# Reciprocal roots of a two-block transformer kernel: a power on GpSimd in the place of ScalarE's root and VectorE's reciprocal

## The chip, the cores and the metric

The kernel runs on one core of a Trainium2 chip. The time is that of one execution on the device, in microseconds (us), and the median of several runs is compared. TensorE (PE in the profile) multiplies and transposes, VectorE (DVE) and ScalarE (ACT) work on rows of 128 partitions, GpSimd (POOL) does small work and issues some loads, and SyncE (SP) issues the loads of the weights. All of them read and write the on-chip SBUF; PE's products land in PSUM. ACT evaluates a function from a table, and an ACT_TABLE_LOAD stands ahead of a function whose table isn't the one in place.

## The reference

Input are 256 tokens of width 1024, in fp32. A first block (one layer) mixes them by attention, by a long convolution (hyena) and by a Fourier branch, adds a mixture of 16 experts where each expert picks its top 32 tokens, and ends in a norm. A second block follows, of two layers. Every norm is of this form:

```python
def rms_norm(x, g):
    y = x * lax.rsqrt(jnp.mean(x * x, axis=-1, keepdims=True) + EPS)
    return y * g

def second_block(...):
    for i in range(2):
        f = swiglu(rmsnorm(h, g[0]), gate[i, 0], up[i, 0], down[i, 0])
        h = h + 0.5 * rmsnorm(f, g[1])
        mix = hybrid_mixer(rmsnorm(h, g[2]), ...)
        h = h + rmsnorm(mix, g[3])
        f = swiglu(rmsnorm(h, g[4]), gate[i, 1], up[i, 1], down[i, 1])
        h = h + 0.5 * rmsnorm(f, g[5])
        gate_ = sigmoid(rmsnorm(h, g[6]) @ w_ple_gate[i])
        h = h + rmsnorm((p[i] @ w_ple[i]) * gate_, g[7])
```

In the first block `qk_heads` norms each head of 64, the router works on the norm of the residual, and in the second block's mixer the latents (256 and 128 wide) and both groups of the attention output (512 wide) are normed too.

## The kernel before

Tokens stand on the partitions, in two halves of 128. Weights stream from HBM in 1 MB tiles through a ring of slots that SP refills. Except in the experts, a product keeps fp32 accuracy by splitting each operand in a high and a low part: `wsplit` copies a piece of 128 x 1024 of a weight on ACT (`wh`, line 1137) and subtracts on DVE (`wl`, line 1138), or on POOL for the first eight pieces of the second block, and `mm3` (lines 163 to 165) multiplies three times.

The first mixer runs to about 300 us; `head_norm` (line 484) norms the heads, and beside it POOL multiplies by the rope's cosines (`ho`, line 497). The router follows, half by half (line 798): ACT squares the residual and sums (`sqj`, 814), takes the root (`rr`, 816), DVE its reciprocal (817); ACT takes the exponential of the logits (`affw`, 830), and x times `rr` (`x1h`, `xs`, 896 and 897) is what the tokens are gathered from. The top 32 of each expert are found from `affw`, then the tokens are gathered, and the products of the experts begin, for which 384 loads of 1 MB stream in to 1256 us. A first Sqrt of one element (`warm`, line 972) follows the last expert's Silu.

The second block is eight sublayers long: FFN, mixer, FFN and embedding gate (PLE), twice. Each ends in `rows_linear` (line 1202), whose first half of the tokens ends eight weight tiles before the second, so that the chain of norms of one half runs beside the products of the other. For a half, `between` (line 1181) does this:

- ACT squares the result and sums (`ns`, 1155), DVE multiplies by the gain (`nt`, 1194), ACT takes the root (1158 or 1160), DVE the reciprocal (1161)
- DVE adds it to the residual (`x`, 1195)
- `pre_norm_half` (1164) repeats it for the next norm: Square (1155), product with the gain (1169), root and reciprocal; then DVE scales the rows in two pieces (1172), PE transposes them (eight `tr`, 1175), ACT and DVE split them into `hh` and `hl` (1178, 1179)

Lines 1011 and 1013 add the experts' result and apply the first block's last norm. At the very end `last_half` (line 1336) treats the second half's result by columns; its root is warmed by a Sqrt of one element (line 1353). Each engine works its instructions in a fixed order, which the scheduler of the build chose from estimated times; where a cost changes, it places instructions anew. POOL's instructions are in one queue, in which subtractions, loads of gains (`gain`, line 1073) and rope products stand together.

Of the kernel before, what the change touches and what calls it, by code (L numbers as in the profile page):

```python
# [11 lines left out]
F32 = mybir.dt.float32  # L12
F32R = mybir.dt.float32r
I32 = mybir.dt.int32
AF = mybir.ActivationFunctionType
# [18 lines left out]
def _constants():  # L34
# [3 lines left out]
    # rows of the axial rope, interleaved pairs  # L38
# [6 lines left out]
    # implicit filter features and decay  # L45
# [9 lines left out]
    # real DFT of 512 points on 256 samples: cos | -sin with the Nyquist row in the place of sin 0  # L55
# [13 lines left out]
    # 2-d DFT of the Fourier branch, ortho  # L69
# [9 lines left out]
    # masks of the second block: causal, and ln of the number of dilated windows that hold a pair  # L79
# [24 lines left out]
class Builder:  # L104
# [28 lines left out]
    def slot(self, i, nm, dt=F32):  # L133
        """one of the two halves of what becomes the experts' tokens"""
# [5 lines left out]
    def load(self, view, src):  # L140
        """next tile of the weight stream"""
# [25 lines left out]
    def rstd(self, pool, ss, n, width, tag="rs"):  # L167
        """1 / sqrt(ss / width + eps) of a [128, n] tile"""
        nc = self.nc
        r = pool.tile([128, n], F32, name=tag, tag=tag)  # L170
        nc.scalar.activation(r, ss, AF.Sqrt, bias=self.eps, scale=1.0 / width)
        nc.vector.reciprocal(r, r)
        return r

    def sumsq(self, pool, junk, src, n_out=1, tag="ss"):
        nc = self.nc
        s = pool.tile([128, 1], F32, name=tag, tag=tag)
        nc.scalar.activation(junk, src, AF.Square, accum_out=s)
        return s

    def sin_reduced(self, pool, r, x, shape, tag):
        """r = x reduced to [-pi, pi] by multiples of 2 pi"""
# [12 lines left out]
    def run(self):  # L195
# [7 lines left out]
        nc.vector.memset(self.eps, EPS)  # L203
        self.ones = P.tile([128, 128], F32, name="ones")
# [25 lines left out]
    def first_mixer(self, st):  # L230
        nc, tc, A = self.nc, self.tc, self.A
        P, M, ident = self.P, self.M, self.ident
        # left: what lives to the end of the phase | the middle's operands; right: tokens | branches
# [28 lines left out]
        # small vectors as rows, then as columns  # L262
# [29 lines left out]
        # silu of both conditionings; 16 equal columns each  # L292
# [5 lines left out]
        # modulation: columns of 2048 at a time, four column tiles of the array at once  # L298
# [36 lines left out]
        # norms of x and ctx, transposed  # L335
        def norm_T(src, dst, scaled):
            for h in range(2):
                xn = scaled(h)
                s = self.sumsq(L, xn, src[:, h])
                r = self.rstd(L, s, 1, D)  # L340
# [8 lines left out]
        def affine(i, src, hi, lo):  # L349
            """src (1 + scale) g + shift, split"""  # L350
# [22 lines left out]
        # affine of the norms: A = g (1 + sc), B = sh  # L373
# [22 lines left out]
        # implicit filters  # L396
# [22 lines left out]
        # spectra: A = re, B = im (row 0 zero), Dm = re with the Nyquist row first; [f, (order, w)]  # L419
# [11 lines left out]
        # 1 / sum |filter|, channels on the partitions  # L431
# [10 lines left out]
        # rope tables with the gains of q and k  # L442
# [15 lines left out]
        def by_k(w):  # L458
            """pieces of a [128, 8, 256] chunk for products with the tokens on the rows"""
# [23 lines left out]
        def head_norm(src, nh):  # L483
            """rms norm over 64 of each of nh heads, [128, nh, 64] in PSUM"""
            sq = H1.tile([128, 8, 64], F32, name="hsq", tag="hsq", bufs=1)
            nc.scalar.activation(sq[:, :nh], src, AF.Square)
            ss = H1.tile([128, 8], F32, name="hss", tag="hss", bufs=2)
            nc.vector.tensor_reduce(ss[:, :nh], sq[:, :nh], axis=AX.X, op=OP.add)
            r = self.rstd(L, ss[:, :nh], nh, 64, tag="hr%d" % nh)
# [15 lines left out]
        def twice(nh, o, t):  # L505
            """o + t, each head two times, for transposes that fill the lower and the upper rows"""
# [73 lines left out]
        # hyena columns: padded, short convolution  # L580
# [12 lines left out]
        # Fourier columns  # L593
# [3 lines left out]
        # operands of the branch products: attention 4, hyena 2, Fourier 2  # L597
# [15 lines left out]
        # attention over 256 + 256 keys, heads i of both groups together  # L613
# [39 lines left out]
        # hyena: two long convolutions  # L653
# [41 lines left out]
        # Fourier mix  # L695
# [41 lines left out]
        # gates and branches, 256 features at a time; the other modulations in between  # L737
# [37 lines left out]
        # router weights with the gain of norm 2, and what its shift brings to the logits  # L775
# [12 lines left out]
        # output product, half by half  # L788
# [9 lines left out]
        def router(h):  # L798
            """the residual, and the affinities of its norm to the experts"""
# [14 lines left out]
            nc.scalar.activation(junk, x[:, h], AF.Square, accum_out=s)  # L814
            r = rr[h] = B.tile([128, 1], F32, name="rr", tag="rr", bufs=2)
            nc.scalar.activation(r, s, AF.Sqrt, bias=self.eps, scale=1.0 / D)
            nc.vector.reciprocal(r, r)
# [35 lines left out]
        # operands of the gather: they outlive this phase a little  # L853
# [816 lines left out]
```

## Time and profile before

| | us |
|---|---|
| runs: median (lowest to highest) | 2371.19 (2369.87 to 2372.92) |
| profiled execution: span | 2373.4 |
| PE busy | 1985.2 (84%) |
| DVE busy | 924.2 (39%) |
| ACT busy | 768.6 (32%) |
| POOL busy | 94.9 (4%) |
| mean DMA rate | 276 GB/s |

The profiled execution took as long as the slowest of the runs. The shares are of the whole span, through which three stretches run with different limits; so the rows further down are taken stretch by stretch. In them a line gives the start and the length of an instruction, then engine, line of the kernel, operation, what is written and what is read, and in square brackets how long the engine had been idle and who released it.

### The profile page before, as it was taken

The page shows a single profiled execution, that of the slowest core. Times are in us where ns is not written, and L with a number is a line of the kernel's source. Part 1 is how long each engine was busy: PE and PEld are TensorE (multiplying, and loading weights), DVE is VectorE, ACT ScalarE, POOL GpSimd, SP SyncE. Part 2 cuts the span into 40 slices and gives each one's busy share as a digit, 9 for nine tenths or more (in the row PEclk, how much of TensorE's full clock was granted, in tenths as well). Part 3 has the DMA queues.
Part 4 walks back from the last instruction along what each step waited for, and adds up shares of the span by engine and source line. Part 5 has one row for each costly group of instructions (what it writes and reads, how often), then busy time and mean ns, then how long its engine had stood idle before and what let it go on. Part 6 is the DMA issues. An engine that isn't in the chain of part 4 may idle for free.

```text
span 2373.4 us, 32208 instructions
## 1 busy us (share of the span) xinstructions
PE 1985.2 (84%) x13512; PEld 1344.9 (57%) x13512; DVE 924.2 (39%) x1535; ACT 768.6 (32%) x1235; POOL 94.9 (4%) x110
## 2 busy tenths in 40 slices
PE   7899977666666666666666999999999999999998
PEld 4778932111111111111114998879987998879986
DVE  5855530100000000000005555676547554777545
ACT  5544420000000000000003444576436544666444
POOL 2100010000000000000003000100000000110000
PEclk9999987767766776677677999999999999999999
DMA  9466699999999999999996654437556554536551
GB/s 327 151 230 215 248 358 417 416 416 417 417 417 416 417 416 417 417 417 416 417 417 218 213 179 155 154 113 228 179 185 205 178 194 141 172 127 196 178 194 64
DMA packets 234869, 655.78 MB, mean 276 GB/s; under 512 B 12663, under 2 KB 143140, under 8 KB 198884
## 3 DMA queue, kind: packets, MB, share of 16 engines
q1 hardware_dynamic: 230436, 639.00, 71.6%
q0 software_dynamic: 4288, 14.72, 1.9%
q8 instruction: 106, 1.74, 0.3%
q14 instruction: 39, 0.32, 0.0%
HBM read 650.54 MB, written 3.15 MB: 275 GB/s over the span
## 4 chain that ended last, share of the span: by engine, by line
PE 55%; DMA 37%; DVE 4%; ACT 3%; issue 1%; SPq 0%; DVEq 0%; POOL 0%; ACTq 0%; POOLq 0%
DMA wt<-in_w_up_dram 24%; DMA wt<-in_w_down_dram 12%; PE gu L163 8%; PE gu L165 8%; PE gu L164 8%; PE acc L163 5%; PE acc L165 5%; PE acc L164 5%; PE gu L942 2%; PE mm L163 2%; PE mm L165 1%; PE mm L164 1%; PE mod L310 1%; ACT wh L1137 1%; PE gu L1593 1%
## 5 line engine op out<-in xcount | busy, mean ns | idle before, releaser
L1138 DVE TENSOR_TENSOR wl<-wt,wh 128x1024 fp32r<-128x1024 f32 (+1 forms) x380 | 462.6, 1223 | 295.9 <-ACT wh L1137 295.1
L942 PE MATMUL gu<-wt,xg 128*32 128x512 f32 x2048 | 392.0, 860 | 190.3 <-DMA wt<-in_w_up_dram 97.5
L1137 ACT ACTIVATE wh<-wt 128x1024 fp32r<-128x1024 f32 x388 | 404.6, 1051 | 302.9 <-PE gu L164 118.6
L942 PEld LDWEIGHTS gu<-wt,xg 128*32 128x32 f32 x2048 | 50.5, 126 | 517.0 <-DMA wt<-in_w_up_dram 231.6
L163 PE MATMUL gu<-hh,wh 128*128 128x256 f32 x1152 | 326.3, 283 | 0.0
L164 PE MATMUL gu<-hl,wh 128*128 128x256 f32 x1152 | 326.0, 283 | 0.0
L165 PE MATMUL gu<-hh,wl 128*128 128x256 f32 x1152 | 326.0, 283 | 0.0
L967 ACT ACTIVATE a<-gu 128x512 f32<-128x512 f32 x16 | 9.6, 597 | 865.6 <-PE gu L942 865.6
L990 PE MATMUL tr<-wt,aT 128*32 128x256 f32 x2048 | 193.0, 525 | 96.7 <-DMA wt<-in_w_down_dram 84.1
L973 DVE TENSOR_TENSOR a<-a,gu 128x512 f32<-128x512 f32 x16 | 11.0, 688 | 561.6 <-PE gu L942 559.5
L164 PEld LDWEIGHTS gu<-hl,wh 128*128 128x128 f32 x1152 | 221.1, 192 | 0.0
L165 PEld LDWEIGHTS gu<-hh,wl 128*128 128x128 f32 x1152 | 221.1, 192 | 0.0
L163 PEld LDWEIGHTS gu<-hh,wh 128*128 128x128 f32 x1152 | 221.1, 192 | 0.0
L990 PEld LDWEIGHTS tr<-wt,aT 128*32 128x32 f32 x2048 | 71.2, 140 | 211.7 <-DMA wt<-in_w_down_dram 142.7
L163 PE MATMUL acc<-wh,ah 128*128 128x512 f32 x352 | 139.8, 397 | 0.0
L165 PE MATMUL acc<-wh,al 128*128 128x512 f32 x352 | 139.6, 396 | 0.0
L164 PE MATMUL acc<-wl,ah 128*128 128x512 f32 x352 | 139.5, 396 | 0.0
L995 DVE TENSOR_TENSOR y<-tr,g2b 32x256 f32<-32x256 f32 x64 | 26.9, 420 | 278.3 <-PE tr L990 277.6
L163 PE MATMUL acc<-wh,hh 128*128 128x256 f32 (+1 forms) x304 | 102.4, 337 | 1.1 <-ACT vd L1408 1.1
L163 PE MATMUL gu<-wh,hh 128*128 128x256 f32 (+1 forms) x336 | 99.8, 298 | 0.4 <-ACT hh L1178 0.4
L165 PE MATMUL acc<-wh,hl 128*128 128x256 f32 (+1 forms) x304 | 99.6, 328 | 0.0
L164 PE MATMUL acc<-wl,hh 128*128 128x256 f32 (+1 forms) x304 | 99.1, 326 | 0.0
(456 smaller groups left out, 2889.7 us busy)
## 6 DMA issues: line engine op xcount, KB each, us to landing
wt<-in_w_gate_dram SPq DMA_DIRECT2D x128, 1024.0 KB, 19.8
wt<-in_w_up_dram SPq DMA_DIRECT2D x128, 1024.0 KB, 19.9
wt<-in_w_down_dram SPq DMA_DIRECT2D x128, 1024.0 KB, 20.0
wt<-in_ffn_gate_dram SPq DMA_DIRECT2D x44, 1024.0 KB, 6.3
wt<-in_ffn_up_dram SPq DMA_DIRECT2D x44, 1024.0 KB, 5.4
wt<-in_ffn_down_dram SPq DMA_DIRECT2D x44, 1024.0 KB, 4.9
wt<-in_w_in_dram SPq DMA_DIRECT2D x35, 1024.0 KB, 5.4
wt<-in_w_mod_dram SPq DMA_DIRECT2D x24, 1024.0 KB, 8.5
```

Of the source, the lines that this page charges most:

```text
L163: mm(out, lw[0], rw[0], start=start, stop=False, skip_group_check=skip)
L164: mm(out, lw[0], rw[1], start=False, stop=False, skip_group_check=skip)
L165: mm(out, lw[1], rw[0], start=False, stop=stop, skip_group_check=skip)
L310: last = mm(ps[32 * j:32 * j + 32, :], cst[:, k].rearrange("p a b -> p (a b)"), w[:, 512 * j:512 * j + 512], start=(k == 0), stop=(k == KD ...
L942: mm(ps[32 * j:32 * j + 32, :], xg[k][:, 32 * e:32 * e + 32], w[:, 512 * j:512 * j + 512], start=(k == 0), stop=(k == KD - 1), skip_group_ ...
L967: silu = nc.scalar.activation(a, pga, AF.Silu)
L973: mul = nc.vector.tensor_tensor(a, a, pup, op=OP.mult)
L990: mm(pd[32 * c:32 * c + 32, :256], aT[:, b, 32 * j:32 * j + 32], w[:, i, 256 * c:256 * c + 256], start=(t == 0), stop=(t == 15), skip_grou ...
L995: nc.vector.tensor_tensor(y4[32 * r:32 * r + 32, 256 * c:256 * c + 256], pd[32 * c:32 * c + 32, :256], self.g2b[32 * c:32 * c + 32, 256 * ...
L1137: nc.scalar.activation(hi, src, AF.Copy)
L1138: (eng or nc.vector).tensor_tensor(lo, src, hi.bitcast(F32), op=OP.subtract)
L1593: mm(p[:, e * i:e * i + e], q(n0 + i, h), k(n0 + i, e), start=True, stop=True, skip_group_check=True)
```

## The change

All norms but the group norm of the mixer (its root, line 1547, stays on ACT) take their reciprocal root on POOL. A new function does it in two instructions, an add of epsilon and a power with the exponent -0.5 from a constant tile:

```diff
+    def root(self, r, ms, eps=EPS):
+        self.nc.gpsimd.tensor_scalar(r, ms, eps, None, op0=OP.add)
+        self.nc.gpsimd.tensor_tensor(r, r, self.mhalf[:, :r.shape[-1]], op=OP.pow)
...
+        self.mhalf = P.tile([128, 8], F32, name="mhalf")
+        nc.vector.memset(self.mhalf, -0.5)
...
     def norm_rstd(self, src, junk, width, half=False):
+        f = 2.0 if half else 1.0
-        nc.scalar.activation(junk, src, AF.Square, accum_out=s)
+        nc.scalar.activation(junk, src, AF.Square, scale=f * width ** -0.5, accum_out=s)
-            nc.scalar.activation(r, s, AF.Sqrt, bias=self.eps4, scale=4.0 / width)
...
-            nc.scalar.activation(r, s, AF.Sqrt, bias=self.eps, scale=1.0 / width)
-        nc.vector.reciprocal(r, r)
+        self.root(r, s, f * f * EPS)
...
-            nc.scalar.activation(sq[:, :nh], src, AF.Square)
+            nc.scalar.activation(sq[:, :nh], src, AF.Square, scale=0.125)
...
-            nc.scalar.activation(r, s, AF.Sqrt, bias=self.eps, scale=1.0 / D)
-            nc.vector.reciprocal(r, r)
+            self.root(r, s)
...
-                    nc.scalar.activation(warm, self.eps, AF.Sqrt)
...
-                nc.scalar.activation(s[:, 2:3], self.eps, AF.Sqrt)
...
-            nc.scalar.activation(s[:, 3:4], s[:, 0:1], AF.Sqrt, bias=self.eps, scale=1.0 / D)
+            self.root(s[:, 3:4], s[:, 0:1])
             nc.vector.tensor_tensor(t[:, cs], t[:, cs], g[:, cs], op=OP.mult)
-            nc.vector.reciprocal(s[:, 3:4], s[:, 3:4])
```

The division by the width goes into the scale of the Square. In the order of ACT 50 roots and the two of one element are gone, and 25 ACT_TABLE_LOADs stand where 48 stood; on DVE 50 reciprocals are gone; on POOL 100 instructions are new. Other instructions move, since the scheduler places them anew.

On ACT, in the second half of the router (`sqj` the square of the residual, `rr` the root, `affw` the exponential, `x1h` and `xs` the rows for the gather), it read:

```order
L814 ACTIVATE sqj,rss<-x_70 128x1024
L816 ACT_TABLE_LOAD
L816 ACTIVATE rr<-rss,eps 128x1
L897 ACTIVATE xs<-x_70,rr 128x1024
L830 ACT_TABLE_LOAD
L830 ACTIVATE affw,rsum<-lg,rm 128x16
L896 ACTIVATE x1h<-x_70,rr 128x1024
L897 ACTIVATE xs<-x_70,rr 128x1024
```

and reads now:

```order
L815 COPY xt<-tr 128x512
L818 ACTIVATE sqj,rss<-x_72 128x1024
L900 ACTIVATE xs<-x_72,rr 128x1024
L899 ACTIVATE x1h<-x_72,rr 128x1024
L833 ACTIVATE affw,rsum<-lg,rm 128x16
L900 ACTIVATE xs<-x_72,rr 128x1024
```

The root and the table loads around it are gone, and the rows for the gather go ahead of the exponential.

On POOL, where the second block begins (`wl` the subtractions for the first weights, `gain` loads of norm gains), it read:

```order
L1029 DMA grows<-in_norm_gains_dram 1x16x64
L1138 TENSOR_TENSOR wl<-wt,wh 128x1024 x7
L1073 DMA gain<-in_norm_gains_dram 128x1024
L1138 TENSOR_TENSOR wl<-wt,wh 128x1024
L1073 DMA gain<-in_norm_gains_dram 128x1024
```

and reads now, the roots of the four norms of this place between them:

```order
L1027 DMA grows<-in_norm_gains_dram 1x16x64
L1134 TENSOR_TENSOR wl<-wt,wh 128x1024 x2
L169 TENSOR_SCALAR nr<-ns 128x1
L170 TENSOR_TENSOR nr<-nr,mhalf 128x1
L1134 TENSOR_TENSOR wl<-wt,wh 128x1024 x2
L169 TENSOR_SCALAR nr<-ns 128x1
L170 TENSOR_TENSOR nr<-nr,mhalf 128x1
L169 TENSOR_SCALAR nr<-ns 128x1
L170 TENSOR_TENSOR nr<-nr,mhalf 128x1
L1134 TENSOR_TENSOR wl<-wt,wh 128x1024
L1069 DMA gain<-in_norm_gains_dram 128x1024
L1134 TENSOR_TENSOR wl<-wt,wh 128x1024
```

The first root stands behind two subtractions and the next two behind four; the last of the four comes after this piece.

On DVE, at the border of the second FFN of layer 0 and the PLE product, the first half of the tokens (`nt` the rows, `nr` the reciprocal root, `wl` subtractions of the running product's weights), it read:

```order
L1194 TENSOR_TENSOR nt<-acc,gain 128x1024
L1161 RECIPROCAL nr<-nr 128x1
L1195 SCALAR_TENSOR_TENSOR x_70<-nt,nr,x_70 128x1024
L1138 TENSOR_TENSOR wl<-wt,wh 128x1024
L1169 TENSOR_TENSOR nt<-x_70,gain 128x1024
L1138 TENSOR_TENSOR wl<-wt,wh 128x1024
L1161 RECIPROCAL nr<-nr 128x1
L1138 TENSOR_TENSOR wl<-wt,wh 128x1024
L1172 TENSOR_SCALAR nt<-nt,nr 128x512 x2
L1138 TENSOR_TENSOR wl<-wt,wh 128x1024 x2
```

and reads now:

```order
L1187 TENSOR_TENSOR nt<-acc,gain 128x1024
L1188 SCALAR_TENSOR_TENSOR x_72<-nt,nr,x_72 128x1024
L1134 TENSOR_TENSOR wl<-wt,wh 128x1024
L1162 TENSOR_TENSOR nt<-x_72,gain 128x1024
L1134 TENSOR_TENSOR wl<-wt,wh 128x1024
L1165 TENSOR_SCALAR nt<-nt,nr 128x512 x2
L1134 TENSOR_TENSOR wl<-wt,wh 128x1024
```

The reciprocals are gone, and the scaling of the rows has one subtraction fewer ahead of it. In PE's order the eight transposes that follow it have moved ahead of 8 matmuls of the running product here; at the other borders of the second block they moved by 8 to 10 matmuls ahead in seven more halves, by one in two, and not at all or behind up to 8 in the others.

## Rows read from the trace of the kernel before

**Rows 1.** Windows: busy time of each engine and instructions, granted clock, DMA share, GB/s

```profile
300.00:1256.00 956.00, 635.92 (x4277) 151.96 (x4277) 69.01 (x159) 28.01 (x46) 9.22 (x11) 0.71 1.01 414
...
1256.00:2373.00 1117.00, 1075.45 (x7316) 972.68 (x7316) 676.56 (x1011) 594.34 (x964) 61.72 (x60) 0.98 0.52 171
```

**Rows 2.** Waits of PE, 1256 to 2374 us: total us, times, longest us

```profile
PE tr L1175 <- DVE nt L1172: 17.6, 5, 10.5
```

**Rows 3.** Groups by line: busy us, mean ns, then idle before

```profile
L1160 ACT ACTIVATE nr<-ns,eps 128x1 f32<-128x1 f32 x25 | 7.2, 286 | 0.3
...
L1161 DVE RECIPROCAL nr<-nr 128x1 f32<-128x1 f32 x33 | 5.2, 156 | 4.9 <-ACT nr L1160 3.4 <-ACT nr L1158 1.5
```

**Rows 4.** Timeline, first mixer: start us, duration us, instruction, count

```profile
20.41 1.28 ACT L405 ACT_TABLE_LOAD   x1
...
59.79 2.14 POOL L497 TENSOR_TENSOR ho<-hn,tabc 128x512 f32<-128x512 f32 x1 [8.72 <-issue]
```

**Rows 5.** Timeline: small POOL instructions, and the DVE ones beside them

```profile
47.02 3.70 DVE L1138 TENSOR_TENSOR wl<-wt,wh 128x1024 fp32r<-128x1024 f32 x3
...
47.04 1.32 POOL L454 TENSOR_TENSOR tabs<-k_ropes,gains 128x32 f32<-128x32 f32 x1
...
50.80 0.26 POOL L454 TENSOR_TENSOR tabs<-k_ropes,gains 128x32 f32<-128x32 f32 x1
...
299.77 0.19 POOL L861 COPY gaff<-aff 128x8 f32<-128x8 f32 x1 [126.95 <-DVE yt L805]
```

**Rows 6.** Timeline of ACT in the second half of the router

```profile
303.43 1.28 ACT L816 ACT_TABLE_LOAD   x1
...
304.93 1.13 ACT L897 ACTIVATE xs<-x,rr 128x1024 f32<-128x1024 f32 x1
...
307.37 0.31 ACT L830 ACTIVATE affw<-lg,rm 128x16 f32<-128x16 f32 x1
```

**Rows 7.** Window ahead of the experts' stream

```profile
319.00:323.00 4.00, 4.00 (x24) 1.51 (x20) 0.00 (x0) 0.46 (x1) 0.00 (x0) 0.56 0.50 152
```

**Rows 8.** Timeline from the experts into the second block: POOL, DVE, PE

```profile
1267.02 11.40 POOL L1138 TENSOR_TENSOR wl<-wt,wh 128x1024 fp32r<-128x1024 f32 x4 [1.51 <-ACT wh L1137]
...
1273.84 4.87 DVE L1172 TENSOR_SCALAR nt<-nt,nr 128x512 f32<-128x512 f32 x2
...
1276.36 1.09 PE L1175 MATMUL tr<-ident,nt 128*128 128x128 f32 x4 [10.55 <-DVE nt L1172]
...
1287.87 1.38 PE L1175 MATMUL tr<-ident,nt 128*128 128x128 f32 x8 [2.43 <-DVE nt L1172]
```

**Rows 9.** Timeline, gate product into the next layer: ACT, DVE, PE

```profile
1815.91 1.28 ACT L1160 ACT_TABLE_LOAD   x1
...
1817.73 1.28 DVE L1195 SCALAR_TENSOR_TENSOR x<-nt,nr,x 128x1024 f32<-128x1024 f32 x1
...
1824.16 1.77 PE L1175 MATMUL tr<-ident,nt 128*128 128x128 f32 x8 [3.20 <-DVE nt L1172]
```

**Rows 10.** Timeline: POOL in the mixer, and one half border of the second block

```profile
1478.49 1.84 POOL L1515 MEMSET qz<- 128x2048 f32 x1
...
1786.95 1.28 ACT L1158 ACT_TABLE_LOAD   x1
...
1786.97 1.22 DVE L1194 TENSOR_TENSOR nt<-acc,gain 128x1024 f32<-128x1024 f32 x1 [10.07 <-ACT nt L1155]
...
1788.77 1.28 DVE L1195 SCALAR_TENSOR_TENSOR x<-nt,nr,x 128x1024 f32<-128x1024 f32 x1
...
1794.58 0.87 DVE L1172 TENSOR_SCALAR nt<-nt,nr 128x512 f32<-128x512 f32 x2
...
1795.46 1.04 PE L1175 MATMUL tr<-ident,nt 128*128 128x128 f32 x8
```

**Rows 11.** Timeline of DVE at the end

```profile
2367.51 0.68 DVE L1357 TENSOR_TENSOR nt<-nt,gain 128x512 f32<-128x512 f32 x1
...
2368.37 1.41 DVE L1361 SCALAR_TENSOR_TENSOR x<-nt,ls,x 128x512 f32<-128x512 f32 x2
```

More of the change, by code (lines that the diff above doesn't have):

```diff
@@ L165, in mm3, with rstd, meansq @@
         mm(out, lw[1], rw[0], start=False, stop=stop, skip_group_check=skip)
-    def rstd(self, pool, ss, n, width, tag="rs"):
-        nc = self.nc
+    def root(self, r, ms, eps=EPS):
+        self.nc.gpsimd.tensor_scalar(r, ms, eps, None, op0=OP.add)
+        self.nc.gpsimd.tensor_tensor(r, r, self.mhalf[:, :r.shape[-1]], op=OP.pow)
+    def rstd(self, pool, ms, n, tag="rs"):
         r = pool.tile([128, n], F32, name=tag, tag=tag)
-        nc.scalar.activation(r, ss, AF.Sqrt, bias=self.eps, scale=1.0 / width)
-        nc.vector.reciprocal(r, r)
-        return r
-    def sumsq(self, pool, junk, src, n_out=1, tag="ss"):
-        nc = self.nc
+        self.root(r, ms)
+        return r
+    def meansq(self, pool, junk, src, tag="ss"):
         s = pool.tile([128, 1], F32, name=tag, tag=tag)
-        nc.scalar.activation(junk, src, AF.Square, accum_out=s)
+        self.nc.scalar.activation(junk, src, AF.Square, scale=D ** -0.5, accum_out=s)
         return s
@@ L338, in norm_T @@
                 xn = scaled(h)
-                s = self.sumsq(L, xn, src[:, h])
-                r = self.rstd(L, s, 1, D)
+                r = self.rstd(L, self.meansq(L, xn, src[:, h]), 1)
                 nc.vector.tensor_scalar(xn, src[:, h], r, None, op0=OP.mult)
@@ L485, in head_norm @@
             sq = H1.tile([128, 8, 64], F32, name="hsq", tag="hsq", bufs=1)
-            nc.scalar.activation(sq[:, :nh], src, AF.Square)
+            nc.scalar.activation(sq[:, :nh], src, AF.Square, scale=0.125)
             ss = H1.tile([128, 8], F32, name="hss", tag="hss", bufs=2)
             nc.vector.tensor_reduce(ss[:, :nh], sq[:, :nh], axis=AX.X, op=OP.add)
-            r = self.rstd(L, ss[:, :nh], nh, 64, tag="hr%d" % nh)
+            r = self.rstd(L, ss[:, :nh], nh, tag="hr%d" % nh)
             n = H1.tile([128, 8, 64], F32, name="hn", tag="hn", bufs=1)
@@ L813, in router @@
             junk = B.tile([128, D], F32, name="sqj", tag="xt", bufs=2)
-            nc.scalar.activation(junk, x[:, h], AF.Square, accum_out=s)
+            nc.scalar.activation(junk, x[:, h], AF.Square, scale=D ** -0.5, accum_out=s)
             r = rr[h] = B.tile([128, 1], F32, name="rr", tag="rr", bufs=2)
-            nc.scalar.activation(r, s, AF.Sqrt, bias=self.eps, scale=1.0 / D)
-            nc.vector.reciprocal(r, r)
+            self.root(r, s)
             p = tps()
@@ L967, in moe @@
             silu = nc.scalar.activation(a, pga, AF.Silu)
-            if e == NE - 1:
-                warm = self.G.tile([128, 1], F32, name="warm")
-                with tc.issue_after(silu.ins):
-                    nc.scalar.activation(warm, self.eps, AF.Sqrt)
             mul = nc.vector.tensor_tensor(a, a, pup, op=OP.mult)
@@ L1058, in rest @@
             nc.vector.tensor_copy(self.gcol, p[:, :16])
-            self.eps4 = C.tile([128, 1], F32, name="eps4")
-            nc.vector.memset(self.eps4, 4.0 * EPS)
             self.fg, self.g0 = [C.tile([128, D], F32, name="gain", tag="gain", bufs=2) for _ in range(2)]
@@ L1153, in norm_rstd @@
         nc = self.nc
+        f = 2.0 if half else 1.0
         s = self.G.tile([128, 1], F32, name="ns", tag="ns", bufs=4)
-        nc.scalar.activation(junk, src, AF.Square, accum_out=s)
+        nc.scalar.activation(junk, src, AF.Square, scale=f * width ** -0.5, accum_out=s)
         r = self.G.tile([128, 1], F32, name="nr", tag="nr", bufs=4)
-        if half:
-            nc.scalar.activation(r, s, AF.Sqrt, bias=self.eps4, scale=4.0 / width)
-        else:
-            nc.scalar.activation(r, s, AF.Sqrt, bias=self.eps, scale=1.0 / width)
-        nc.vector.reciprocal(r, r)
+        self.root(r, s, f * f * EPS)
         return r
@@ L1344, in tail @@
             cs = slice(512 * c, 512 * c + 512)
-            sig = nc.scalar.activation(t[:, cs], acc, AF.Sigmoid)
+            nc.scalar.activation(t[:, cs], acc, AF.Sigmoid)
             nc.vector.tensor_tensor(t[:, cs], t[:, cs], pw[:, cs], op=OP.mult)
             if c == 0:
-                nc.scalar.activation(fg[:, cs], t[:, cs], AF.Square, accum_out=s[:, 0:1])
+                nc.scalar.activation(fg[:, cs], t[:, cs], AF.Square, scale=D ** -0.5, accum_out=s[:, 0:1])
                 nc.gpsimd.tensor_tensor(t[:, cs], t[:, cs], g[:, cs], op=OP.mult)
                 return
-            with self.tc.issue_after(sig.ins):
-                nc.scalar.activation(s[:, 2:3], self.eps, AF.Sqrt)
-            nc.vector.tensor_tensor_reduce(fg[:, cs], t[:, cs], t[:, cs], 1.0, 0.0, OP.mult, OP.add, s[:, 1:2])
+            nc.vector.tensor_tensor_reduce(fg[:, cs], t[:, cs], t[:, cs], 1.0 / D, 0.0, OP.mult, OP.add, s[:, 1:2])
             nc.vector.tensor_tensor(s[:, 0:1], s[:, 0:1], s[:, 1:2], op=OP.add)
-            nc.scalar.activation(s[:, 3:4], s[:, 0:1], AF.Sqrt, bias=self.eps, scale=1.0 / D)
+            self.root(s[:, 3:4], s[:, 0:1])
             nc.vector.tensor_tensor(t[:, cs], t[:, cs], g[:, cs], op=OP.mult)
-            nc.vector.reciprocal(s[:, 3:4], s[:, 3:4])
             for c in range(2):
@@ L1437, in mixer @@
                     nc.scalar.activation(junk[:, a:b], z[:, h, a:b], AF.Square, scale=(b - a) ** -0.5, accum_out=ss[:, i:i + 1])
-                nc.scalar.activation(ss, ss, AF.Sqrt, bias=self.eps, scale=1.0)
-                nc.vector.reciprocal(ss, ss)
+                self.root(ss, ss)
                 for i, (a, b) in enumerate(((0, 256), (256, 384))):
```

## The prediction

> **What bounds the kernel now.** I read the stretches first, because the share of busy time over the whole span mixes three regimes. Up to about 300 us runs the first mixer, in which TensorE, VectorE and ScalarE take turns. From 300 to 1256 us the experts run, and there the DMA share is 1.01: the weight stream sets the time, and nothing that an engine saves counts unless it lets the stream start earlier [rows 1]. From 1256 us on the second block runs, with TensorE busy 1075.45 of 1117 us [rows 1]; some 40 us of idle time are all that any change off TensorE can win there. The waits of TensorE say whose they are: 17.6 us in five waits on the scaled rows that a norm writes (line 1172), 10.5 of them in one [rows 2]. So the prize in the second block is those 17.6 us; most of the sixteen places where a norm feeds TensorE (two halves at each of eight borders) show no wait at all. The price is read from the groups: a root's ACTIVATE takes 286 ns, a VectorE reciprocal 156 ns [rows 3], and a table load, where one is needed, 1.28 us [rows 4].
>
> **What the change takes away and adds.** 50 roots lose their ACTIVATE and reciprocal; the order of ScalarE holds 25 table loads where it held 48, so 23 go, 23 x 1.28 = 29.5 us, with 50 x 0.29 = 14.5 us of roots, all of it ScalarE's. ScalarE is off the path nearly everywhere, so only the places below count. GpSimd gets 100 small instructions. The 1/width factor moves into the Square, which runs anyway, at no cost.
>
> **What one root costs.** No row shows a power. The add is like the 128x8 copy, 0.19 us; a 128x32 TENSOR_TENSOR alone takes 0.26 us, and the same instruction that meets VectorE's 1024-wide subtractions (two SBUF operands, 1.23 us each) takes 1.32 us [rows 5]. These are my bounds for the power: 0.26 below, 1.32 above. It is a power and not a product, so I take 0.4, near the undisturbed row. A root is then about 0.2 + 0.4 = 0.6 us undisturbed, and up to 2.9 if each of its two instructions first waits out a VectorE one. Before it was 0.29 + 0.16 with the hops between, about 0.5, and 1.8 with a table load. So a place gains about 1.2 us only if it had a load on its path, and else loses 0.1.
>
> The second bound has a rule behind it that speaks against the change: the Trainium skill, SBUF — State Buffer, "SBUF: two separate sides", says that GpSimd and a VectorE operation with two SBUF inputs take a shared port pair as an exclusive lock, the loser waiting for the other's whole instruction. The 1.32 us of that row agrees with it. If it held for both instructions of every root, the time would be that of the second rival below.
>
> **A, first mixer.** At 20.41 us a table load precedes the sine on which TensorE waits [rows 4]; without it some 0.4 us are won before TensorE is full. In the head norms the root, now 8 wide, shares GpSimd with rope products of up to 2.14 us [rows 4] and VectorE has its own products meanwhile; six roots, 0.1 us each by the price above and as much again for the queue: some +0.7 in all. Together +0.3 (-1.5 to +2.5).
>
> **B, router.** In the second half, the root's load (303.43), the root, a row product (304.93, 1.13 us) and another load stand on ScalarE ahead of the exponential at 307.37 [rows 6]. The new order has two such row products there and no load: 303.43 + 2 x 1.13 = 305.7, 1.7 us earlier; the 0.6 us of the root pass beside the first product. The choice of the experts' tokens follows, and the weight stream waits for it: from 319 to 323 us the DMA share is 0.50, a hole of 4 x 0.5 = 2.0 us [rows 7]. Since the stream sets the time from there to 1256, what closes the hole is won whole: -1.7 (-2.0 to +0.5).
>
> By the Trainium skill, ScalarE: Activation LUTs, "What ACT_TABLE_LOAD costs", a switch takes 2.66 us, drain included, and 23 of them 61 us. No drain shows here: the next ACTIVATE starts 0.02 us behind the load. The sum goes by 1.28, and B could not gain more than its hole by either figure.
>
> **C, from the experts into the second block.** TensorE idles 10.55 us before the first transposes and 2.43 us before the second [rows 8]. In between GpSimd does eight subtractions for the first weights, four of them 11.40 us, and VectorE's two scalings of line 1172 that run beside them take 4.87 us [rows 8], against 0.87 elsewhere [rows 10]. The new roots stand in the same GpSimd queue behind two subtractions each, which would cost; but when GpSimd has just finished a root, VectorE's scaling is uncontended. For the first half: GpSimd takes up its second pair of subtractions near 1267.0 as before, two at 11.40 / 4 = 2.85 us end at 1272.7, the root behind them at 1273.3, and half of the scaling, 0.44 to 1.2 us, lets the transposes start at about 1274.4 instead of 1276.36. The second half, with the same two queues, moves by about the same, 1287.87 to 1285.9. C gives -2.0 (-4.5, the scaling wholly free and no wait behind subtractions, to +1, each root behind a 2.85 us subtraction).
>
> **D, gate into the next layer's first product (1810 to 1836).** Here TensorE idles 3.20 us, and the chain holds a table load at 1815.91 with its root, after which the residual starts at 1817.73 [rows 9]. The sum of squares is there at 1815.9 without the load; with a 0.6 root the residual starts at about 1816.6. That saves 1.1, and the second root's reciprocal no longer stands between VectorE's subtractions, some 0.4 more: -1.5 (-2.5 to +1).
>
> **E, the other thirteen halves.** TensorE is full there and nothing can be won, but the new order puts the eight transposes earlier into TensorE's queue, by 8 to 10 matmuls of 0.23 us (1.86 to 2.33) in eight of them, so the chain must hurry. Take one [rows 10]. Before: sum ready where the load starts, 1786.95; residual 1788.77; scaling 1794.58; transposes 1795.46. After: the product with the gain (1786.97 + 1.22) holds the residual until 1788.2, so the first root has 1.25 us and hides. Behind the residual VectorE has one subtraction fewer, 1.2: scaling at 1788.2 + (1794.58 - 1788.77) - 1.2 = 1792.8. The transposes are due at 1795.46 - 1.86 = 1793.6 and need half of the scaling, 0.44: 0.3 us to spare. The second root has from about 1790.6 to 1792.8, 2.2 us; undisturbed it needs 0.6, and with each instruction behind a VectorE one 2.9, which is 0.7 late and, less the 0.3, a stall of 0.4. I take 0.12 on average: 13 x 0.12 = +1.5 (0 to 13 x 0.4 = +5). In the mixer the GpSimd queue holds a 1.84 us MEMSET ahead of a root [rows 10], which is in that allowance.
>
> **F, the end.** The last root leaves ScalarE for GpSimd beside VectorE's 0.68 us product; VectorE's last step started at 2368.37, 0.18 behind the end of that product [rows 11]. A 0.6 root from 2367.5, if it waits for the product, ends at 2368.75: +0.4 (0 to +1.2).
>
> **Sum.** 0.3 - 1.7 - 2.0 - 1.5 + 1.5 + 0.4 = -3.0 us. The profiled span, 2373.4, is 2.2 above the median of the runs, 2371.19; I apply the difference in us to the median: 2368.2.
>
> **Rivals.** First, **faster**: GpSimd finds gaps between VectorE's instructions, E costs nothing, and C takes its lower bound because VectorE escapes GpSimd's subtractions: 0 - 2 - 4.5 - 2 + 0 + 0.2 = -8.3, 2362.9. For it: C's 4.87 against 0.87. Against: the 1.32 us row.
> Second, **slower**: the lock holds at every border, so that a stall follows the power one to one. With a power of p us each of the thirteen halves loses what its second root takes, 1.1 + 0.2 + 1.2 + p, less the 2.2 and the 0.3 to spare: p, and A to D and F sum to -4.5 + 4 (p - 0.4). At p = 0.4 that is +0.7, at p = 1.0 it is 13 - 2.1 = +11, 2382. It decides from about p = 0.65. For it: the 1.32 us row. Against: the undisturbed GpSimd rows, 0.19 and 0.26.
> Third, **no effect**: B's hole is filled by a later wait of the stream, and C's roots stand behind subtractions, so A to F cancel: 2371 to 2372.
>
> **How the numbers follow.** Forecast 0.42, faster rival 0.25, slower rival 0.2, no effect 0.13. 0.2% is 4.7 us, about what a measurement of this kernel tells from no change: the bounds are 2366.4 and 2375.9. Of the forecast's spread about a quarter lies below the lower one: faster 0.25 + 0.1 = 0.35; slower 0.2 and a little of the forecast's own, 0.22; within 0.43. The range reaches down past the faster rival's time to 2361 and up to 2380, short of the slower rival's worst; the forecast's own range is 2364 to 2372.
>
> **What would show it.** In the changed kernel: power rows on GpSimd of 0.3 to 0.5 us, in twos with the add; the stream's hole near 320 us almost closed; the first transposes near 1274; TensorE's idle time ahead of transposes at the thirteen borders, 0.1 to 0.2 each. It is wrong if powers take over 0.65 us and stalls of half a microsecond stand at each border (then slower), or if the experts' end does not move by B.

## The result, and the profile after

The changed kernel is slower: 2394.75 us (median of four runs, 2393.69 to 2394.85) against 2370.53 before (2371.19 ahead of the prediction was the median of three of these four runs), a ratio of 1.0101 with an interval of 1.0088 to 1.0113, or +24.2 us. The forecast was -3.0 us, and its range ended at 2380; the measured time lies beyond even the second rival's 2382, which it had for a power of 1 us.

From 1256 us on TensorE has nearly the busy time that it had, 1082.67 us in a stretch that is now 1136 us long; in [rows 1] it was 1075.45 of 1117. The two windows aren't quite the same work, since the last expert's last product starts at 1269.1 us now and at 1258.1 before. The window of the changed kernel, with the columns of that group:

```profile
1256.00:2392.00 1136.00, 1082.67 (x7396) 974.12 (x7388) 674.28 (x973) 568.36 (x910) 120.12 (x136) 0.98 0.51 172
```

The groups of GpSimd's new instructions (busy us, mean ns | idle before), which the kernel before has none of; a root's ACTIVATE and reciprocal were 286 and 156 ns [rows 3]:

```profile
L170 POOL TENSOR_TENSOR nr<-nr,mhalf 128x1 f32<-128x1 f32 x33 | 26.4, 801 | 2.6
...
L169 POOL TENSOR_SCALAR nr<-ns 128x1 f32<-128x1 f32 x33 | 25.9, 784 | 796.9 <-ACT nt L1152 796.6
...
L170 POOL TENSOR_TENSOR hr<-hr,mhalf 128x8 f32<-128x8 f32 x2 | 4.2, 2105 | 0.2
...
L170 POOL TENSOR_TENSOR hr<-hr,mhalf 128x2 f32<-128x2 f32 x4 | 3.1, 770 | 0.3
```

An add took 0.78 us in the mean and a power 0.80, where the prediction had 0.2 and 0.4; a power of eight columns took 2.1 us. TensorE's waits on the scaled rows (total us, times, longest) show where it went in the second block, here from 1300 us on, after the way into it; of the five waits in the whole block before, 17.6 us [rows 2], two stand there. The changed kernel, and the one before:

```profile
PE tr L1168 <- DVE nt L1165: 9.7, 12, 2.3
```

```profile
PE tr L1175 <- DVE nt L1172: 3.4, 2, 3.2
```

Since one profiled execution scatters by some 3 us, the time is split between fixed points of TensorE's work, and compared with every profile whose code is the same as before in that stretch. The column of the old code is a mean of such profiles, those of the experiments below among them (where there are two, both are given); that of the changed kernel is its one profile:

| stretch, from TensorE's work to TensorE's work | old code, us (profiles) | changed kernel, us | difference | forecast |
|---|---|---|---|---|
| start to the first product with the attention's values | 114.0 (4, 112.6 to 115.4) | 129.5 | +15.4 | A: +0.3 |
| on to the first output product | 157.9 (4) | 157.8 | -0.1 | 0 |
| on to the last expert's last product | 983.8 (2, 983.3 and 984.4) | 981.8 | -2.0 | B: -1.7 |
| on into the first FFN of the second block | 50.2 (3, 49.4 to 50.9) | 51.9 | +1.7 | C: -2.0 |
| on to the end | 1062.2 (3, 1061.1 to 1064.3) | 1071.9 | +9.7 | D, E, F: +0.4 |

The differences add up to 24.7 us, against 24.2 measured. In the last stretch the profile of the kernel before was itself the longest of the three.

**The first mixer** lost in three places. At the start the first product of the modulation now stands ahead of the transposes of x in TensorE's queue, and waits for its weight (PE of the changed kernel, then of the one before):

```profile
11.92 1.88 PE L315 MATMUL mod<-wt,cst 128*32 128x512 f32 x2 [7.14 <-DMA wt<-in_w_mod_dram]
...
13.73 0.48 PE L349 MATMUL tr<-ident,xn 128*128 128x128 f32 x1
```

```profile
8.19 1.11 PE L345 MATMUL tr<-ident,xn 128*128 128x128 f32 x4 [3.03 <-DVE xn L341]
...
11.17 1.89 PE L310 MATMUL mod<-wt,cst 128*32 128x512 f32 x5 [1.01 <-DMA wt<-in_w_mod_dram]
```

The transposes of x, ready at about 8 us as before, start at 13.73. A good part of that is caught up later; 2.7 us are left when the first product with the weights starts. Then the head norms. The timeline of VectorE and GpSimd for the first two:

```profile
59.81 1.23 DVE L1134 TENSOR_TENSOR wl<-wt,wh 128x1024 fp32r<-128x1024 f32 x1 [0.26 <-ACT wh L1133]
...
60.03 2.54 POOL L170 TENSOR_TENSOR hr<-hr,mhalf 128x8 f32<-128x8 f32 x1
...
62.60 0.69 DVE L495 TENSOR_TENSOR hn<-pq,hr 128x512 f32<-128x512 f32 x1 [1.57 <-POOL hr L170]
...
65.14 1.67 POOL L170 TENSOR_TENSOR hr<-hr,mhalf 128x8 f32<-128x8 f32 x1
```

The power of eight columns takes 1.67 us alone, and 2.54 where it meets a subtraction that started just before it; VectorE idles 1.57 us for it. Over the head norms and the products behind them 5.9 us are lost. And in the attention, ScalarE and TensorE:

```profile
118.58 1.28 ACT L634 ACT_TABLE_LOAD   x1
...
122.22 0.69 PE L648 MATMUL tr<-ident,ae 128*128 128x128 f32 x2 [5.54 <-DVE ae L636]
...
122.54 0.61 ACT L667 ACTIVATE zt<-tr 128x512 f32<-128x512 f32 x1
```

The copy `zt`, on which the hyena branch's products wait, is behind four exponentials and their table load, and on TensorE the transposes of those exponentials stand ahead of these products: 5.54 us of idle time. Before, the copy came first, and TensorE waited 1.74 (0.69 in the three other profiles with the old code there):

```profile
109.19 0.59 ACT L663 ACTIVATE zt<-tr 128x512 f32<-128x512 f32 x1
...
109.79 1.28 ACT L630 ACT_TABLE_LOAD   x1
...
109.82 1.35 PE L670 MATMUL mm<-zt,dft 128*128 128x256 f32 x5 [1.74 <-ACT zt L663]
```

From the first attention score to the first product with the attention's values the changed kernel takes 15.25 us where the one before took 9.78. Of the 5.5 us, 3.8 are idle time; the rest goes with a lower clock: the granted clock was 0.79 from 114 to 130 us, in which the 5.54 us of idle time lie, and 1.00 (the level of 2.4 GHz) from 106 to 115 us before.

**The router** did as forecast. ScalarE has no load between the sum of squares and the exponential, 2.32 us apart now, where [rows 6] had 3.94 from the root's load to it:

```profile
316.83 0.19 ACT L818 ACTIVATION_READ_ACCUMULATOR sqj<-x 128x1 f32 x1
...
319.15 0.29 ACT L833 ACTIVATE affw<-lg,rm 128x16 f32<-128x16 f32 x1
```

**A half border of the second block**, the one of [rows 10], on VectorE, GpSimd and TensorE:

```profile
1802.97 1.22 DVE L1187 TENSOR_TENSOR nt<-acc,gain 128x1024 f32<-128x1024 f32 x1 [10.09 <-ACT nt L1152]
...
1803.04 0.22 POOL L169 TENSOR_SCALAR nr<-ns 128x1 f32<-128x1 f32 x1 [172.46 <-ACT nt L1152]
...
1803.34 0.57 POOL L170 TENSOR_TENSOR nr<-nr,mhalf 128x1 f32<-128x1 f32 x1
...
1806.64 1.22 DVE L1162 TENSOR_TENSOR nt<-x,gain 128x1024 f32<-128x1024 f32 x1
...
1806.86 1.07 POOL L169 TENSOR_SCALAR nr<-ns 128x1 f32<-128x1 f32 x1 [2.94 <-ACT nt L1152]
...
1807.77 1.22 DVE L1134 TENSOR_TENSOR wl<-wt,wh 128x1024 fp32r<-128x1024 f32 x1
...
1808.01 1.40 POOL L170 TENSOR_TENSOR nr<-nr,mhalf 128x1 f32<-128x1 f32 x1
...
1809.45 0.88 DVE L1165 TENSOR_SCALAR nt<-nt,nr 128x512 f32<-128x512 f32 x2 [0.45 <-POOL nr L170]
...
1810.08 1.06 PE L1168 MATMUL tr<-ident,nt 128*128 128x128 f32 x8 [0.42 <-DVE nt L1165]
```

The first root meets a product that reads PSUM and SBUF (1802.97): the add takes 0.22 us and the power 0.57. The second root meets operations with two SBUF operands: its add starts at 1806.86 and ends 0.07 us after the product that was running (1806.64 + 1.22), its power starts just behind the next subtraction's start and ends 0.42 after that one's end. So VectorE's scaling waits 0.45 us, and TensorE 0.42, ahead of transposes that the new order wants early.

### The profile page after: what moved, and what is told of

It is laid out like the page before. It is cut to its first block, busy times and chain, and to the rows that moved or that the text cites. A ratio compares the mean times of both kernels' runs of the same rounds, so it can differ in the third digit from the quotient of the medians.

```text
span 2392.8 us, 32236 instructions
## 1 busy us (share of the span) xinstructions
PE 1987.9 (83%) x13512; PEld 1346.0 (56%) x13512; DVE 921.9 (39%) x1485; ACT 728.8 (30%) x1160; POOL 164.2 (7%) x210
## 3 DMA queue, kind: packets, MB, share of 16 engines
q8 instruction: 106, 1.74, 0.3%
## 4 chain that ended last, share of the span: by engine, by line
PE 49%; DMA 37%; DVE 3%; ACT 3%; POOL 2%; issue 1%; DVEq 0%; POOLq 0%; SPq 0%; ACTq 0%
DMA wt<-in_w_up_dram 25%; DMA wt<-in_w_down_dram 11%; PE gu L163 7%; PE gu L165 7%; PE gu L164 7%; PE acc L163 5%; PE acc L165 5%; PE acc L164 5%; PE gu L945 2%; PE mm L163 1%; PE mm L165 1%; PE mm L164 1%; ACT wh L1133 1%; PE gu L1581 1%; POOL nr L170 1%
## 5 line engine op out<-in xcount | busy, mean ns | idle before, releaser
L165 PE MATMUL gu<-wh,hl 128*128 128x256 f32 (+1 forms) x336 | 99.3, 297 | 3.5 <-DVE hl L1172 3.5
L164 PE MATMUL gu<-wl,hh 128*128 128x256 f32 (+1 forms) x336 | 99.5, 297 | 0.0
```

Source lines behind the costliest of these rows:

```text
L164: mm(out, lw[0], rw[1], start=False, stop=False, skip_group_check=skip)
L165: mm(out, lw[1], rw[0], start=False, stop=stop, skip_group_check=skip)
```

## The experiments

In the diffs, `root_act` is ScalarE's root and VectorE's reciprocal.

**Half of the change at a time.** The first kernel keeps the power in the first block only:

```diff
-        self.root(r, s, f * f * EPS)
+        self.root_act(r, s, self.eps4 if half else self.eps)
...
-                self.root(ss, ss)
+                self.root_act(ss, ss)
...
-            self.root(s[:, 3:4], s[:, 0:1])
+            nc.scalar.activation(s[:, 3:4], s[:, 0:1], AF.Sqrt, bias=self.eps, scale=1.0)
```

> The power on GpSimd in the first block alone (norms of x and of the context, heads, router); the second block and the last norm keep ScalarE's root and VectorE's reciprocal, with both warm-ups. Theory A (two trace readings: TensorE's and ScalarE's order changed in the first mixer, and 8-wide powers in the head norms): the first mixer loses 14 us, the router gives back 3, the second block is as before: +11 us against the kernel before. Rival B (the loss is what the slower rival of the prediction said, at the borders of the second block alone): 0 to -3 us.

The second kernel does the reverse:

```diff
-        self.root(r, ms)
+        self.root_act(r, ms)
...
-            self.root(r, s)
+            self.root_act(r, s)
             p = tps()
```

> The power on GpSimd in the second block and the last norms alone; the first mixer, heads and router keep root and reciprocal. Theory A: borders lose 8, the way into the second block 1, the gate border wins 1, the end loses 0.6: +8 to +9 us against the kernel before. Rival B: all of the loss, +19 to +24 us.

Measured: the first block alone 2379.07 us, 1.0037 (1.0024 to 1.0050) or +7.8; the second block alone 2380.22, 1.0039 (1.0024 to 1.0054) or +8.9. Rival B is out, since neither half carries the whole: by the times each has a third of the loss or a little more. Theory A had the second right and the first 3 us too high, just inside its interval. The halves sum to 16.7 and not to 24.2; their intervals, some 3 us to either side each, leave room for most of the difference, and the stretches say the same in both kernels as in the changed one (128.1 us to the attention's values, 1071.1 at the end), so no interaction is needed, though none is excluded. The waits of the second kernel from 1300 us on are those of the changed kernel again:

```profile
PE tr L1172 <- DVE nt L1169: 9.5, 12, 2.2
```

**A product in the place of the power**, in the same order on every engine, with 0.001 in the constant tile:

```diff
-        self.nc.gpsimd.tensor_tensor(r, r, self.mhalf[:, :r.shape[-1]], op=OP.pow)
+        self.nc.gpsimd.tensor_tensor(r, r, self.mhalf[:, :r.shape[-1]], op=OP.mult)
```

> The changed kernel with the power replaced by a product with 0.001 on the same engine, in the same order on every engine; so no norm is a norm any more, and the difference to the changed kernel is what a power takes over a product. Theory A1 (the power's own length, 0.57 us alone and 1.7 to 2.5 us for 8 columns, counts): product of 0.2 us, head norms win 4 us, thirteen borders 0.37 each, C, D and F 1.5: -10 us against the changed kernel, +10 to +14 against the one before. Theory A2 (waiting for VectorE's operations counts, whatever the instruction does): 0 to -3 us against the changed kernel.

Measured: 2380.72 us, 1.0041 (1.0026 to 1.0056): 14 us less than the changed kernel. So the length of the power counts, more than theory A1 had (-10). But it doesn't stand alone. The groups and the waits of this kernel:

```profile
L169 POOL TENSOR_SCALAR nr<-ns 128x1 f32<-128x1 f32 x33 | 24.2, 732 | 798.7 <-ACT nt L1152 798.4
...
L170 POOL TENSOR_TENSOR nr<-nr,mhalf 128x1 f32<-128x1 f32 x33 | 14.8, 449 | 2.6
```

```profile
PE tr L1168 <- DVE nt L1165: 2.5, 3, 1.5
```

The add is as long as before, 0.73 us, and the product still takes 0.45 in the mean, where it takes 0.19 alone: the waiting for VectorE is the same. At the border above it takes 1.03 us where the power took 1.40, and of the twelve waits three are left; that of the way into the second block, 1.50 us, now lies just ahead of 1300. So waiting and length are one budget: a stall is what is over it. The first mixer kept the attention's 5.7 us of idle time, and lost 2.1 us in the head norms instead of 5.9.

**The old order at two places**, by telling the scheduler what to issue after what:

```diff
-            mod_last = mod_step(0, k)
+            with tc.issue_after(self.xt0.ins) if k == 0 else nullcontext():
+                mod_last = mod_step(0, k)
...
-        att_scores(0)
+        zt0 = hy_zt(0)
+        with tc.issue_after(zt0[1].ins):
+            att_scores(0)
```

Here `xt0` is the last of the first eight transposes of x, and `hy_zt` the transposes and the copy `zt`.

> The changed kernel with two places of the old order forced: the first product of the modulation behind the first eight transposes of x on TensorE, and the copy zt of the hyena branch ahead of the first exponentials of the attention on ScalarE. Theory A (the order, not the roots, costs there): the start wins 2.7 us and the attention 5.5, -8 us against the changed kernel, +12 to +16 against the one before. Rival C (whoever is late there waits for something else next, a load or a buffer): 0 to -3 us against the changed kernel.

Measured: 2389.48 us, 1.0076 (1.0059 to 1.0093), 5.3 us less than the changed kernel, where theory A had 8. In the trace the stretch to the attention's values is 123.0 us and not 129.5: 2.5 won at the start, 4.2 in the attention, 0.2 lost between them. So the order costs 6.5 of the 15.4 us there, and rival C holds for about a fifth of what theory A claimed.

**The power without the add**: epsilon is left out of these norms.

```diff
-        self.nc.gpsimd.tensor_scalar(r, ms, eps, None, op0=OP.add)
-        self.nc.gpsimd.tensor_tensor(r, r, self.mhalf[:, :r.shape[-1]], op=OP.pow)
+        self.nc.gpsimd.tensor_tensor(r, ms, self.mhalf[:, :r.shape[-1]], op=OP.pow)
```

> The changed kernel without the add: the power is taken of the mean square itself, so epsilon (1e-6) is left out of these norms. One GpSimd instruction a root instead of two. Theory A2 (each GpSimd instruction that meets a VectorE operation with two SBUF operands waits for its end, so a root at a border pays two such waits, 1.08 and 1.40 us): one wait is gone, the root fits into the 2.2 us that the border has, the stalls of 0.4 to 0.5 us go: -8 to -10 us against the changed kernel, +14 to +16 against the one before. Theory A1 (the length of the power alone counts): the add is 0.22 us, some fifteen of them lie on the path: -3 us.

Measured: 2380.63 us, 1.0038 (1.0024 to 1.0051), 14.1 less, more than theory A2 had (8 to 10). That is far more than fifteen adds of 0.22 us: at a border an instruction less is a wait less. From 1300 us on:

```profile
PE tr L1167 <- DVE nt L1164: 4.7, 5, 1.5
```

Twelve waits of 9.7 us became five of 4.7, and the last stretch went from 1071.9 to 1065.6. The way into the second block became 1.7 us longer. The rest was won in the first mixer, 10.0 us to the attention's values: the first two powers there took 1.65 and 1.83 us, the first clear of the subtraction that it met before, and the head norms lost 0.6 us instead of 5.9. Part of that is another order on the engines, which this kernel also has; the two weren't separated.

**The head norms back on ScalarE and VectorE**, the other 44 roots on GpSimd:

```diff
-            r = self.rstd(L, ss[:, :nh], nh, tag="hr%d" % nh)
+            r = self.rstd(L, ss[:, :nh], nh, tag="hr%d" % nh, act=True)
```

> The changed kernel with the six roots of the head norms on ScalarE and VectorE as before; all others on GpSimd. In its order the copy zt stands ahead of the exponentials again, as in the kernel before; the start keeps the changed order. Theory A: the head norms win 6 us (8-wide powers of 1.67 and 2.54 us, and the queue) and the attention 5: -10 to -12 us against the changed kernel, +12 to +14 against the one before; the products of the attention start within 3 us of before. Rival C: -3 us.

Measured: 2381.60 us, 1.0045 (1.0031 to 1.0058), 13.2 less (theory A had 10 to 12); six of fifty roots carried more than half of the loss: 6.4 us were won in the head norms and 4.1 in the attention, whose order came with them. In this kernel the copy stands ahead again, and the wait is 2.12 us, where the kernel before had 1.74:

```profile
111.66 1.77 PE L678 MATMUL mm<-zt,dft 128*128 128x256 f32 x5 [2.12 <-ACT zt L671]
```

**The router alone** on GpSimd, two roots of fifty; all others are on `root_act`.

> Of the change only the two roots of the router are on GpSimd; every other root is on ScalarE and VectorE as before. Theory A (term B of the prediction was right): the exponential comes 1.7 us earlier and closes the hole in the weight stream: -1.5 to -3 us against the kernel before, the first mixer and the second block unchanged. Rival D (the stream finds another wait): within 0.5 us.

Measured: 2367.77 us against 2370.48, a ratio of 0.9984 (0.9975 to 0.9992), or -2.7 us: term B stands, and this version beats both kernels. The window of 4 us that holds its hole (DMA share in the column ahead of the last) is the counterpart of [rows 7], 0.86 now where it was 0.50, so the hole shrank from 2.0 us to 0.6:

```profile
314.00:318.00 4.00, 3.79 (x30) 1.23 (x24) 0.00 (x0) 0.46 (x1) 0.32 (x1) 0.80 0.86 305
```

**The router and all of the second block**, both with the power alone (epsilon left out), the first mixer as before.

> First mixer and head norms on ScalarE and VectorE as before; the router and all of the second block on GpSimd with the power alone (epsilon left out there). Theory A: first mixer as before, router -2, way into the second block 0 to -2, gate border -1, other borders 0 to +2, end 0: -3 us against the kernel before (-5 to +1). Rival A1 (length of the power counts at the borders): +4 to +7.

Measured: 2372.89 us, 1.0008 (0.9999 to 1.0017): no change that can be told; theory A (-3) and rival A1 (+4 to +7) both missed. Against the kernel with the router alone it is 5.1 us longer. The second block gave the router's gain back: the way into it took 53.9 us, 3.7 more than the old code, with a wait of 4.43 us ahead of the second transposes where [rows 8] had 2.43, and the rest took 1063.1, 0.9 more. With one instruction a root and no wait at most borders, the root on GpSimd still gains nothing where TensorE is full.

## Why the prediction was wrong

**A failed, by 15 us, and is the largest error.** The step weighed the start and the head norms and gave the reorderings no term. Three readings were missing. It put the head norms' powers at the price of a one-column power; a power has a part for each column (0.57 us for one, 0.71 for two, 1.67 for eight), while the root and the reciprocal that it replaces hardly grow (0.30 and 0.20 for eight). And it didn't read the new order of TensorE and ScalarE in the first 120 us: one product ahead of x's transposes, four exponentials ahead of one copy. Both could have been read before the run; the first waits for a load that lands at 11 us or later, the second for 4.0 us of work (118.58 to 122.54). The kernel with the old order at these places won 6.5 us of the stretch, the one with the head norms on ScalarE 11.3.

**What one root costs failed by size.** The bounds were 0.26 and 1.32 us for the power and 0.4 was taken; it took 0.57 alone and 1.40 behind a VectorE operation, over the upper bound by a little. The bounds came from products. In the kernel with a product in its place the product takes 0.19 alone and 1.03 where the power takes 1.40: the power is longer by 0.37 or 0.38 in either case.

**E failed by its average, and by the MEMSET.** Its working came out nearly: it gave the second root 2.2 us and found 2.9 and a stall of 0.4 if each of its instructions waits for VectorE, and at the border that it took the trace has 1.07 + 0.08 + 1.40 = 2.55 us and a stall of 0.42. But 0.12 was taken as a mean, as though the waits were a matter of luck. In the trace the add of every second root waits for a VectorE operation with two SBUF operands (1.01 to 1.08 us at all thirteen), the power at seven of them (1.40; at the other six it takes 0.57 to 0.59). Of the 9.7 us in twelve waits, 1.31 is C's (below) and 2.26 D's; ten waits with 6.1 us are E's. Eight of them, 0.36 to 0.50 us and 3.6 in all, are the eight halves whose transposes the new order moved ahead (two of these by 20 of the narrower matmuls, and not by 8 to 10), each near the 0.4 that was its worst case. The other two take 1.27 us each, at the mixer's borders, where the transposes moved by two matmuls only. There the first root stood behind the 1.84 us MEMSET of [rows 10], which the prediction had named and left in the allowance; the residual waits 0.77 us for that root, and the scaling 0.77 for the next one (GpSimd, VectorE, TensorE):

```profile
1490.85 1.83 POOL L1503 MEMSET qz<- 128x2048 f32 x1
...
1494.06 1.28 DVE L1188 SCALAR_TENSOR_TENSOR x<-nt,nr,x 128x1024 f32<-128x1024 f32 x1 [0.77 <-POOL nr L170]
...
1499.02 1.06 PE L1168 MATMUL tr<-ident,nt 128*128 128x128 f32 x8 [1.27 <-DVE nt L1165]
```

With the power alone these two waits stay, 1.48 and 1.47 us of the 4.7; no run takes the MEMSET out of the way. Besides, TensorE's transposes of the mixer's latents `z` wait 1.2 us twice, where before they had no wait worth a row; there was no term for it. So the waits explain 6.1 - 0.9 (D) + 2.4 + 0.6 (F) = 8.2 of the 9.7 us by which the last stretch is longer; the rest, 1.5, is within the scatter of the old code there.

**The rule on the shared ports.** Beside the product that reads PSUM (1802.97) the add took 0.22 us, beside the one with two SBUF operands 1.07. This agrees with the Trainium skill, SBUF — State Buffer, "SBUF: two separate sides": the loser of the shared port pair waits for the whole instruction, and two SBUF inputs are one of the two ways in which a VectorE operation takes the pair. The prediction cited the page and then gave the rule 0.12 of the 0.4 us that it would cost. Its second rival, which took it whole, has the stall of a border as the power's length, 0.57 x 13 = 7.4 us. E came out at 6.1, but only 3.6 of that in eight halves are such stalls; that the sums are near is in part luck.

**C failed by its sign.** Half of the working held: the first half's second root started behind two subtractions at 1284.09, VectorE's scaling was then uncontended, 0.88 us, and the transposes waited 9.07 us where it had been 10.55. But the contention was moved, not removed: GpSimd's other subtractions now run beside VectorE's operations for the second half.

```profile
1284.09 1.08 POOL L169 TENSOR_SCALAR nr<-ns 128x1 f32<-128x1 f32 x1
...
1285.87 0.88 DVE L1165 TENSOR_SCALAR nt<-nt,nr 128x512 f32<-128x512 f32 x2 [0.77 <-POOL nr L170]
...
1286.50 0.88 PE L1168 MATMUL tr<-ident,nt 128*128 128x128 f32 x3 [9.07 <-DVE nt L1165]
...
1291.24 0.58 PE L165 MATMUL gu<-wh,hl 128*128 128x256 f32 x1 [1.95 <-DVE hl L1172]
...
1296.51 4.69 POOL L1134 TENSOR_TENSOR wl<-wt,wh 128x1024 fp32r<-128x1024 f32 x2
...
1296.58 5.30 DVE L1165 TENSOR_SCALAR nt<-nt,nr 128x512 f32<-128x512 f32 x2 [0.94 <-POOL nr L170]
...
1301.64 0.53 PE L1168 MATMUL tr<-ident,nt 128*128 128x128 f32 x3 [1.31 <-DVE nt L1165]
```

The scaling takes 5.30 us where the other half's took 4.87 before [rows 8]. The transposes behind it wait 1.31 us, less than the 2.43 of [rows 8]; what is new is that TensorE waits 1.95 and 1.10 us for `hl`, VectorE's split of the first half's rows, which stands behind a residual and a product of the second half that take 3.37 and 3.93 us beside GpSimd. The second half wasn't worked out; the prediction let it move "by about the same".

Yet in this profile TensorE's idle time in the stretch fell, from 15.8 us to 14.4. Its work took longer, 37.40 us and not 35.09, at a lower clock (the granted clock is the third column from the right; the changed kernel, then the one before):

```profile
1269.10:1320.90 51.80, 37.40 (x220) 31.20 (x213) 35.26 (x32) 22.90 (x32) 26.19 (x18) 0.73 0.57 188
```

```profile
1258.10:1309.00 50.90, 35.09 (x220) 29.80 (x213) 35.22 (x36) 25.14 (x37) 22.21 (x10) 0.77 0.59 188
```

From 1280.3 us, within the wait of 9.07 us, to 1300.7 the granted clock was 0.50, the level of 1.2 GHz. The other three profiles with the same code in this stretch (the second block alone, the old order at two places, the head norms back) took 52.4 to 53.5 us, with 16.6 to 19.5 us of idle time; the loss is 2.5 us in the mean of the four, and how much of it is the clock differs from profile to profile.

**D, F and B.** D: the transposes of the gate border wait 2.26 us and not 3.20 [rows 9], 0.9 won of the 1.5 forecast, because the powers meet VectorE here too.

```profile
1832.46 1.40 POOL L170 TENSOR_TENSOR nr<-nr,mhalf 128x1 f32<-128x1 f32 x1
...
1839.69 0.56 PE L1168 MATMUL tr<-ident,nt 128*128 128x128 f32 x3 [2.26 <-DVE nt L1165]
```

F: VectorE's last step starts 0.75 us after its product has ended, behind the power, against 0.18 before [rows 11]: +0.57 where +0.4 was forecast.

```profile
2387.19 0.56 POOL L170 TENSOR_TENSOR ls<-ls,mhalf 128x1 f32<-128x1 f32 x1
...
2387.78 1.42 DVE L1350 SCALAR_TENSOR_TENSOR x<-nt,ls,x 128x512 f32<-128x512 f32 x2 [0.75 <-POOL ls L170]
```

B: -1.7 forecast, -2.0 by the stretches (all eight profiles with the router's roots on GpSimd have 981.6 to 982.6 us there, -1.7 in the mean) and -2.7 (0.9975 to 0.9992, about -6 to -2 us) by the run of the router alone. It is the only term in which a table load stood on the path that set the time and nothing on VectorE was in GpSimd's way: the two powers took 0.58 us each.

**The chances.** Slower had 0.22. The rival that came nearest had 0.2, with a power of 0.65 us as the point from which it decides; the power was 0.57, so by its own formula it gave +4 us. Of the remaining 20 us, 15 are A's. The range, worked from the bounds of the same terms, could not hold what had no term.

## What to carry to other kernels

A root that moved to GpSimd cost here its instructions' own time plus, for each instruction, the rest of any VectorE operation with two SBUF operands that it met, and what stood ahead of it in GpSimd's queue. So the number of instructions counts as well as their length: a product in the place of the power won 14.0 us, and one instruction less 14.1, the latter with another order too. The move paid only for roots that stood behind a table load on the path that sets the time and where VectorE was idle; those were two of fifty, worth 2.7 us. And where a scheduler orders the engines anew, read its order all along the stretches that have no slack, for each engine: here two swaps in 120 us cost 6.5 us, more than twice what the two useful roots won.

## What the runs showed of the hardware

A power on GpSimd took 0.57 us for 128x1, 0.71 for 128x2 and 1.67 for 128x8, against 0.19 us for a product, when nothing was in its way. Beside a VectorE operation with two SBUF operands the add ended 0.07 us after that operation, the power 0.42 after it, so that a part of the instruction's own time, 0.15 us of 0.22 and of 0.57, passes while it waits. VectorE itself was not slowed by these small instructions: its subtraction at 1807.77 took 1.22 us, as in [rows 10] its products do.
